# Sample queries in stretches of eight, three state slots, one masked copy a level

## The chip, the cores and the metric

The kernel runs on one core of one Trainium2 chip. The metric is the device time of one execution in microseconds (us), the median of the runs shown. The engines go by the names of the profile: PE (TensorE, the products), PEld (its weight loads), DVE (VectorE), ACT (ScalarE), POOL (GpSimd) and SP (SyncE, which issues most transfers).

## What is computed

One step of a decoder layer with two branches, for a prompt of 256 tokens and for 8 sequences with 4 new tokens each ("samples", 32 tokens), 288 tokens in all. Everything is float32.

```python
h = jnp.einsum('bld,de->ble', x, w_in)            # 2048 -> all projections
# gated linear attention (GLA): 4 heads, keys 256, values 512, a gate for each key
S_t = diag(a_t) S_{t-1} + k_t^T v_t ; o_t = q_t S_t
# retention: 8 heads, keys 128, values 256, one decay gamma a head
S_t = gamma S_{t-1} + k_t^T v_t ; o_t = q_t S_t
merged = sigmoid(ga) * rms(o_a) * silu(za) + sigmoid(gb) * groupnorm(o_b) * silu(zb)
y = jnp.einsum('ble,ed->bld', merged, w_out)
x_new = layer_norm(ALPHA * x + y)
```

The prompt starts from a zero state. The samples start from states that are inputs (16 GLA quads and 8 retention quads of 1 MB each in this kernel's layout), and the new states of both are outputs.

## The kernel before, in words

**The weight stream.** `w_in` is cut into 128 blocks of 128 columns, `w_out` into 16. A block is two halves of 512 KB. Each half is loaded by SyncE (line 228), split into a high and a low float32r part by ACT (line 244) and VectorE (line 245), and multiplied with the 288 tokens in three products for each 128 x 128 piece (lines 258 to 260), 48 products a block. Loads run six halves ahead, splits two halves ahead of the products.

**The order.** The program is written in the order in which every engine runs it; engines run in order. The main loop (line 1115) goes through the blocks a quarter (12 products) at a time. Before each quarter it calls `tick()`: every task (a Python generator) whose turn has come emits its next few instructions, and says with `yield n` in how many ticks it wants to go on. So attention work is laid between quarters of the weight stream, and a tick is one quarter. After the tick the next quarter is split, then multiplied. `Ring` hands out buffers in order: `get` waits tick by tick until the oldest buffer of a full ring is closed. The blocks come in four rounds j of 32; a round has the columns of one GLA head and two retention heads.

**GLA of the prompt.** `gla_main` (line 482) makes the 256 x 256 score matrix by levels: for m = 64, 32, ..., 2 the `producer` forms decayed queries `qs` and keys (lines 515 to 536), PE multiplies them (line 623), and `level_in` (line 596) puts the wanted entries into the scores `st` with two masked copies (`copy_predicated`, line 602), one for each of the two token blocks. The last level (m = 1), the diagonal, and the samples' own scores come out of `pairs` (line 542): POOL forms differences of decays and products of q and k, ACT the exponentials, VectorE multiplies them and adds the two key halves of 176 columns (lines 569, 570), POOL adds the two halves of the 288 diagonal columns (line 573) into `u`, and a product with ones sums over the partitions (line 578, 464 columns, f32). One tick later seven masked copies take the result out of PSUM (lines 581 to 592).

**GLA of the samples.** `gla_sample` (line 657) handles four state quads (j, kt, par). For each it forms a masked key tile `km` (VectorE, line 723), waits until the state's load was queued at least six ticks ago (`state_of`, line 287), lets two ticks go by, and multiplies the queries with the state: four products of 32 query columns with 512 state columns, each on its own 32 columns of the array and its own 32 partitions of `pos` (line 729, 128*32 in the profile). A tick later it begins the update: four times a product of `km` with v (line 734, float32r) into a buffer of the ring `po` (two buffers), and one tick later a VectorE operation (line 736) that decays the state and adds. Then `state_store` (line 292) stores the quad two ticks later and frees the slot; `state_loader` (line 277) queues the next load into the freed slot. `ret_sample` (line 873) does the same for retention quads, both halves par of a head in one quad (line 889, 256 columns; updates on lines 895 and 899). The ring `s8` has two slots, each of 8 KB a partition.

Of the kernel before, what the change touches and what calls it, by code (L numbers as in the profile page):

```python
# [14 lines left out]
ALU = mybir.AluOpType  # L15
# [84 lines left out]
def hybrid_step(ctx: ExitStack, tc: tile.TileContext, xT, xp, xs, w, wlra, wlr, cols, wo, lnwb, lnsb, sg, sr, cf, cu, dtab,  # L100
# [20 lines left out]
    S8 = Ring(spool, "s8", 2, [128, 2048])  # L121

    def R(tag, bufs, shape, dtype=F32, pool=None):
        return Ring(pool or apool, tag, bufs, shape, dtype)
# [8 lines left out]
    PU = R("pu", 1, [128, 2, 352])  # L133
    UU = R("uu", 1, [128, 464])
# [17 lines left out]
    SB = R("sb", 2, [128, NT])  # L152
# [329 lines left out]
    def gla_main(g):  # L482
# [31 lines left out]

        def produce(i):
# [4 lines left out]
            for t in range(2):  # L520
# [8 lines left out]
            dv, qv, kv = (x[:, :, 0:SEQ].rearrange("p k (i n h m) -> p k i n h m", i=2, h=2, m=m)  # L529
                          for x in (dd, q, k))  # L530
            for t in range(2):
                dve.tensor_tensor(qs[:, :, 64 * t:64 * t + 64].rearrange("p k (n m) -> p k n m", m=m),  # L532
                                  qv[:, :, t, :, 1 - t, :], dv[:, :, t, :, 1 - t, :], op=ALU.mult)
# [8 lines left out]
        def pairs():  # L542
# [3 lines left out]
            u = yield from UU.get()  # L546
            pf = p[:, :, 0:144]
            cv = c4.rearrange("p k i (n h) -> p k i n h", h=2)
            pool.tensor_tensor(p[:, :, 0:128].rearrange("p k (i n) -> p k i n", i=2), cv[:, :, :, :, 1],
                               cv[:, :, :, :, 0], op=ALU.subtract)  # L550
            cv = cs.rearrange("p k b (n h) -> p k (b n) h", h=2)
            pool.tensor_tensor(p[:, :, 128:144], cv[:, :, :, 1], cv[:, :, :, 0], op=ALU.subtract)
            for r in range(2):
                pool.tensor_tensor(p[:, :, 144 + 16 * r:160 + 16 * r].rearrange("p k (b t) -> p k b t", t=2),
                                   cs[:, :, :, 2:4], bc(cs[:, :, :, r:r + 1], [128, 2, DEC_BATCH, 2]),
                                   op=ALU.subtract)
            yield 1
            act.activation(p[:, :, 0:176], p[:, :, 0:176], AF.Abs)
            act.activation(p[:, :, 0:176], p[:, :, 0:176], AF.Exp, scale=-1.0 / TAU)
            kv = k.rearrange("p k (n h) -> p k n h", h=2)  # L560
            qv = q.rearrange("p k (n h) -> p k n h", h=2)
            for lo, hi, h in ((0, 64, 1), (64, 128, 0), (128, 144, 1)):
                pool.tensor_tensor(p[:, :, 176 + lo:176 + hi], qv[:, :, lo:hi, h], kv[:, :, lo:hi, 1 - h], op=ALU.mult)
            kv, qv = (x[:, :, SEQ:NT].rearrange("p k (b t) -> p k b t", t=DEC_SEQ) for x in (k, q))
            for r in range(2):
                pool.tensor_tensor(p[:, :, 320 + 16 * r:336 + 16 * r].rearrange("p k (b t) -> p k b t", t=2),
                                   qv[:, :, :, 2:4], bc(kv[:, :, :, r:r + 1], [128, 2, DEC_BATCH, 2]), op=ALU.mult)
# [10 lines left out]
            pe.matmul(pt[:, 0:464], lhsT=ones_t, rhs=u, start=True, stop=True)  # L578
            UU.close(u)
            yield 1  # L580
            dve.copy_predicated(st[:, 0:2, :], U("diag").rearrange("p (i t) -> p i t", i=2),
                                pt[:, 0:256].rearrange("p (i t) -> p i t", i=2))
            level_in(len(LEVELS) - 1, pt[:, 288:416])
            dve.copy_predicated(ss[:, 0, :, 0:8], U("sd").rearrange("p (g c) -> p g c", g=4),
# [3 lines left out]
                                pt[:, 416:432].rearrange("p (g n) -> p g n", g=4))  # L588
            sv = ss[:, 0, :, 0:8].rearrange("p g (n h m) -> p g n h m", h=2, m=2)
# [67 lines left out]
    def gla_sample(g):  # L657
# [61 lines left out]
        for kt in range(2):  # L719
            for par in range(2):  # L720
                qd = ("g", j, kt, par)
# [3 lines left out]
                s8 = yield from state_of(qd)  # L725
                s4 = s8.rearrange("p (g c) -> p g c", g=4)
                yield 2
                for gg in range(4):
                    pe.matmul(pos[32 * gg:32 * gg + 32, :], lhsT=qs[:, kt, 2 * gg + par, :], rhs=s4[:, gg, :],  # L729
                              start=kt + par == 0, stop=False)  # L730
                yield 1
                for gg in range(4):
# [3 lines left out]
                    dve.scalar_tensor_tensor(s4[:, gg, :], s4[:, gg, :], ecs[:, kt, gg, par, 3:4], po,  # L736
# [3 lines left out]
                spawn(state_store(s8, og_s[j, kt, par]))  # L740
# [132 lines left out]
    def ret_sample(r):  # L873
        j, kst, qs, vh = r.j, r.kst, r.qs, r.vh
        pos = yield from POS.get()
        for h in range(2):
# [5 lines left out]
            s4 = s8.rearrange("p (a g c) -> p a g c", a=2, g=4)  # L882
            for par in range(2):
# [694 lines left out]
```

## Time and profile before

| | us |
|---|---|
| median of 3 runs (1086.31 to 1088.1) | 1087.24 |
| profiled execution | 1086.71 |
| its span, first to last instruction | 1084.8 |
| PE busy | 1071.0 |
| DVE busy | 712.8 |
| ACT busy | 524.3 |
| POOL busy | 242.1 |

The profile is one execution. Times in its rows are counted from the first instruction. A PE row gives the start of a product and a modelled time until its end; products overlap, so the rows of PE add up to more than the span, and the distance between starts is what a product takes of the engine. A row with x8 is eight instructions without a gap between them; its time goes from the first start to the last end. An f32 product is two PE instructions, a float32r product one. The granted clock of PE is 0.998 of full over the span.

### The profile page before, as it was taken

The numbers are of one execution on the slowest core, as the hardware profiler recorded it, in microseconds if no ns is written. First come the engines' busy times: TensorE is split into PE (matmuls) and PEld (weight loads), VectorE is DVE, ScalarE is ACT, GpSimd is POOL, SyncE is SP. The second block draws the span as 40 slices with busy tenths as digits, with TensorE's granted clock in tenths as the row PEclk, the third lists the DMA queues.
The fourth block names the chain that finished last, engine by engine and source line by source line (L and its number), as shares of the span: only waits on it lengthen the run. The fifth ranks groups of instructions, "written<-read, shape, count | busy, mean of one in ns | idle before, by whom it ended". The sixth has DMA issues, their size and how long they took to land.

```text
span 1084.8 us, 20286 instructions
## 1 busy us (share of the span) xinstructions
PE 1071.0 (99%) x7987; PEld 1024.6 (94%) x7987; DVE 712.8 (66%) x1313; ACT 524.3 (48%) x1054; POOL 242.1 (22%) x345
## 2 busy tenths in 40 slices
PE   9999999999999999999999999999999999999996
PEld 7999999999999999999999999999989999999985
DVE  5758866655568767554578766554588667675557
ACT  6665344444565435344664444345564444453342
POOL 0223212121242213031260212040260221230003
PEclk9999999999999999999999999999999999999999
DMA  9744757575445776675436675664436774655853
GB/s 332 245 160 138 263 198 269 181 265 172 158 137 163 238 245 227 209 246 169 164 119 201 248 249 180 228 239 155 156 117 215 249 270 150 205 193 180 245 185 117
DMA packets 57807, 219.12 MB, mean 202 GB/s; under 512 B 6512, under 2 KB 8432, under 8 KB 51568
## 3 DMA queue, kind: packets, MB, share of 16 engines
q1 hardware_dynamic: 56288, 214.95, 58.4%
q10 hardware_dynamic: 1424, 2.88, 1.0%
q8 instruction: 63, 1.03, 0.4%
q14 instruction: 32, 0.26, 0.1%
HBM read 187.13 MB, written 30.67 MB: 201 GB/s over the span
## 4 chain that ended last, share of the span: by engine, by line
PE 96%; DVE 3%; DMA 0%; issue 0%; POOL 0%; ACT 0%; SPq 0%
PE acc L258 28%; PE acc L260 27%; PE acc L259 27%; PE pos L729 1%; PE po L734 1%; PE pt L309 1%; PE po L416 1%; PE po L414 1%; PE po L415 1%; PE pt L623 1%; PE pos L889 1%; PE po L895 1%; DVE wl L245 1%; DVE y L1348 1%; PE pt L352 0%; PE pt L383 0%
## 5 line engine op out<-in xcount | busy, mean ns | idle before, releaser
L258 PE MATMUL acc<-xh,wh 128*128 128x288 f32 x2240 | 673.9, 301 | 1.1 <-ACT wh L244 1.1
L259 PE MATMUL acc<-xl,wh 128*128 128x288 f32 x2240 | 660.6, 295 | 0.0
L260 PE MATMUL acc<-xh,wl 128*128 128x288 f32 x2240 | 659.5, 294 | 0.2 <-DVE wl L245 0.2
L245 DVE TENSOR_TENSOR wl<-raw,wh 128x512 fp32r<-128x512 f32 x572 | 408.4, 736 | 318.2 <-ACT wh L244 315.9
L244 ACT ACTIVATE wh<-raw 128x512 fp32r<-128x512 f32 x572 | 337.3, 625 | 435.2 <-PE acc L259 397.9
L258 PEld LDWEIGHTS acc<-xh,wh 128*128 128x128 f32 x2240 | 420.6, 188 | 22.4 <-issue 13.7
L259 PEld LDWEIGHTS acc<-xl,wh 128*128 128x128 f32 x2240 | 423.4, 189 | 3.5 <-issue 0.8
L260 PEld LDWEIGHTS acc<-xh,wl 128*128 128x128 f32 x2240 | 422.5, 189 | 0.5 <-DVE wl L245 0.4
L998 POOL TENSOR_TENSOR sg<-sg,sb 128x288 f32<-128x288 f32 x32 | 32.6, 1019 | 277.3 <-ACT sb L996 277.3
L736 DVE SCALAR_TENSOR_TENSOR s<-s,ec,po 128x512 f32<-128x512 f32 x64 | 47.4, 741 | 0.0
L761 POOL TENSOR_TENSOR kq<-t,t 64x288 f32<-64x288 f32 x16 | 15.9, 992 | 107.0 <-DVE t L755 106.4
L522 POOL TENSOR_TENSOR t<-cc 128x256 f32<-128x256 f32 x48 | 36.7, 794 | 0.0
L322 POOL TENSOR_SCALAR sm<-sm 128x1 f32<-128x1 f32 (+1 forms) x24 | 9.0, 376 | 105.7 <-ACT on L340 64.1
L734 PE MATMUL po<-vh,km 128*128 128x512 f32 x64 | 26.1, 408 | 1.8 <-DVE s L736 1.8
L899 DVE SCALAR_TENSOR_TENSOR s<-s,po 128x512 f32<-128x512 f32 x32 | 21.8, 680 | 3.1 <-PE po L895 3.1
L1331 POOL TENSOR_SCALAR mv<-mv 128x1 f32<-128x1 f32 x3 | 1.7, 559 | 96.3 <-DVE mv L1388 94.2
L532 DVE TENSOR_TENSOR qsc<-kq,t 128x128 f32<-128x128 f32 x48 | 22.4, 507 | 0.1
L665 POOL COPY qsp<-qe 128x32 f32<-128x32 f32 x8 | 4.6, 606 | 76.8 <-DVE qe L504 76.8
L470 POOL MEMSET t<- 128x4 f32 x4 | 0.4, 104 | 94.1 <-DVE t L464 77.8
L1206 ACT ACTIVATE y<-pt 128x256 f32<-128x256 f32 x12 | 4.6, 385 | 34.0 <-DVE stt L1203 24.6
L323 POOL TENSOR_TENSOR sm<-sm,cft 128x1 f32<-128x1 f32 (+1 forms) x24 | 19.2, 799 | 2.0
L919 POOL TENSOR_TENSOR merged<-merged,sg 128x288 f32<-128x288 f32 x16 | 15.5, 980 | 8.9 <-DVE merged L358 8.5
(257 smaller groups left out, 994.4 us busy)
## 6 DMA issues: line engine op xcount, KB each, us to landing
raw<-in_w SPq DMA_DIRECT2D x252, 512.0 KB, 4.3
s<-in_sg SPq DMA_DIRECT2D x16, 1024.0 KB, 4.9
out_og_s<-s SPq DMA_DIRECT2D x16, 1024.0 KB, 8.1
raw<-in_wo SPq DMA_DIRECT2D x32, 512.0 KB, 4.7
s<-in_sr SPq DMA_DIRECT2D x8, 1024.0 KB, 4.8
out_or_s<-s SPq DMA_DIRECT2D x8, 1024.0 KB, 6.6
raw<-in_w SPq DMA_DIRECT2D x8, 256.0 KB, 5.6
lnt<-in_lnwb ACTq DMA_DIRECT2D x4, 512.0 KB, 8.5
```

Source lines behind the costliest of these rows:

```text
L244: act.activation(a[:, s], t[:, s], AF.Copy)
L245: (pool if q in POOL_Q else dve).tensor_tensor(b[:, s], t[:, s], a[:, s].bitcast(F32), op=ALU.subtract)
L258: pe.matmul(acc, lhsT=a[:, k, :], rhs=xh, start=first and k == kk, stop=False)
L259: pe.matmul(acc, lhsT=a[:, k, :], rhs=xl, start=False, stop=False)
L260: pe.matmul(acc, lhsT=b[:, k, :], rhs=xh, start=False, stop=last and k == kk + 3)
L323: pool.tensor_tensor(r[:, 0:n], r[:, 0:n], bc(mhalf[:, 0:1], [128, n]), op=ALU.pow)
L522: pool.tensor_tensor(dd[:, :, t * 128:t * 128 + 128].rearrange("p k (n m) -> p k n m", m=2 * m), cv, bc(cv[:, :, :, m - 1 + t:m + t], [128 ...
L532: dve.tensor_tensor(qs[:, :, 64 * t:64 * t + 64].rearrange("p k (n m) -> p k n m", m=m), qv[:, :, t, :, 1 - t, :], dv[:, :, t, :, 1 - t, : ...
L734: pe.matmul(po, lhsT=km[:, gg, :], rhs=vh[:, 2, :], start=True, stop=True)
L736: dve.scalar_tensor_tensor(s4[:, gg, :], s4[:, gg, :], ecs[:, kt, gg, par, 3:4], po, op0=ALU.mult, op1=ALU.add)
L899: dve.scalar_tensor_tensor(sv, sv, g4, po, op0=ALU.mult, op1=ALU.add)
L998: pool.tensor_tensor(gt, gt, s, op=ALU.mult)
```

## The change

Sample queries: `gla_sample` takes the states of both par of one kt first and multiplies eight products in one stretch, before the first `km`; `ret_sample` does the same with the two halves of its quad. The waits of two ticks behind `km` stay, the tick behind the queries goes. The ring `s8` gets a third slot; for that `sb` gets one buffer in place of two, and `u` is dropped.

Levels: `level_in` makes one masked copy of 128 columns in place of two of 64, through a view (`half_view`) that reaches over both token blocks; the decayed queries are laid out for it, split by key half in place of token block.

The ones product: decays and products of `pairs` change places in `p`, which grows to 464 columns; VectorE's addition of 176 columns is dropped and POOL adds all 464; `p` itself is the operand of the ones product and is freed after it. The copies out of PSUM are spread over four ticks.

```diff
-    S8 = Ring(spool, "s8", 2, [128, 2048])
+    S8 = Ring(spool, "s8", 3, [128, 2048])
-    PU = R("pu", 1, [128, 2, 352])
-    UU = R("uu", 1, [128, 464])
+    PU = R("pu", 1, [128, 2, 464])
-    SB = R("sb", 2, [128, NT])
+    SB = R("sb", 1, [128, NT])
...
+        def half_view(ap, m):
+            return ap[:, m:m + 2 * (128 - m)].rearrange("p (i a m) -> p i a m", i=2, m=m)[:, :, ::2, :]
...
-            for t in range(2):
-                dve.tensor_tensor(qs[:, :, 64 * t:64 * t + 64].rearrange("p k (n m) -> p k n m", m=m),
-                                  qv[:, :, t, :, 1 - t, :], dv[:, :, t, :, 1 - t, :], op=ALU.mult)
+            for kt in range(2):
+                dve.tensor_tensor(qs[:, kt].rearrange("p (i n m) -> p i n m", i=2, m=m), half_view(q[:, kt], m),
+                                  half_view(dd[:, kt], m), op=ALU.mult)
...
-            dve.tensor_tensor(p[:, :, 0:176], p[:, :, 0:176], p[:, :, 176:352], op=ALU.mult)
-            dve.tensor_tensor(u[:, 288:464], p[:, 0, 0:176], p[:, 1, 0:176], op=ALU.add)
+            dve.tensor_tensor(dec, dec, qk, op=ALU.mult)
             pool.tensor_tensor(p[:, :, 0:NT], q, k, op=ALU.mult)
             yield 1
-            pool.tensor_tensor(u[:, 0:NT], p[:, 0, 0:NT], p[:, 1, 0:NT], op=ALU.add)
-            PU.close(p)
+            pool.tensor_tensor(p[:, 0], p[:, 0], p[:, 1], op=ALU.add)
             yield 2
             pt = yield from PT.get()
-            pe.matmul(pt[:, 0:464], lhsT=ones_t, rhs=u, start=True, stop=True)
-            UU.close(u)
+            pe.matmul(pt[:, 0:464], lhsT=ones_t, rhs=p[:, 0], start=True, stop=True)
+            PU.close(p)
             yield 1
             dve.copy_predicated(st[:, 0:2, :], U("diag")...
+            yield 1
             level_in(len(LEVELS) - 1, pt[:, 288:416])
+            yield 1
             dve.copy_predicated(ss[:, 0, :, 0:8], U("sd")...
             dve.copy_predicated(sv[:, :, :, 1], U("s1")...
+            yield 1
             for r in range(2):
                 dve.copy_predicated(sv[:, :, :, 1, :], U(f"s2{r}")...
...
         def level_in(i, src):
             m = LEVELS[i]
-            for t in range(2):
-                sv = st[:, t, :].rearrange("p (n h m) -> p n h m", h=2, m=m)
-                mk = U("lev")[:, i * 128 + 64 * t:i * 128 + 64 * t + 64].rearrange("p (n m) -> p n m", m=m)
-                dve.copy_predicated(sv[:, :, 1 - t, :], mk,
-                                    src[:, 64 * t:64 * t + 64].rearrange("p (n m) -> p n m", m=m))
+            sv = half_view(st.rearrange("p i t -> p (i t)"), m)
+            dve.copy_predicated(sv, U("lev")[:, i * 128:i * 128 + 128].rearrange("p (i n m) -> p i n m", i=2, m=m),
+                                src[:, 0:128].rearrange("p (i n m) -> p i n m", i=2, m=m))
...
         for kt in range(2):
+            s8 = []
             for par in range(2):
-                qd = ("g", j, kt, par)
+                t = yield from state_of(("g", j, kt, par))
+                s8.append(t)
+            s4 = [t.rearrange("p (g c) -> p g c", g=4) for t in s8]
+            for par in range(2):
+                for gg in range(4):
+                    pe.matmul(pos[32 * gg:32 * gg + 32, :], lhsT=qs[:, kt, 2 * gg + par, :], rhs=s4[par][:, gg, :],
+                              start=kt + par == 0, stop=False)
+            for par in range(2):
                 km = yield from KM.get()
                 E_KM.tensor_tensor(km, ...
-                s8 = yield from state_of(qd)
-                s4 = s8.rearrange("p (g c) -> p g c", g=4)
                 yield 2
-                for gg in range(4):
-                    pe.matmul(pos[32 * gg:32 * gg + 32, :], lhsT=qs[:, kt, 2 * gg + par, :], rhs=s4[:, gg, :],
-                              start=kt + par == 0, stop=False)
-                yield 1
                 for gg in range(4):
                     po = yield from PO.get()
                     pe.matmul(po, lhsT=km[:, gg, :], rhs=vh[:, 2, :], start=True, stop=True)
                     yield 1
...
             s8 = yield from state_of(qd)
+            for par in range(2):
+                for gg in range(4):
+                    pe.matmul(pos[32 * gg:32 * gg + 32, c], lhsT=qs[:, h, 2 * gg + par, :], rhs=s4[:, par, gg, :],
+                              start=h + par == 0, stop=False)
             for par in range(2):
                 km = yield from KM.get()
                 E_KM.tensor_tensor(km, ...
                 yield 2
-                for gg in range(4):
-                    pe.matmul(pos[32 * gg:32 * gg + 32, c], lhsT=qs[:, h, 2 * gg + par, :], rhs=s4[:, par, gg, :],
-                              start=h + par == 0, stop=False)
-                yield 1
                 for g2 in range(2):
```

## Rows read from the trace of the kernel before

**Rows 1.** The page, its first line and part 1 (busy us, share, instructions)

```profile
span 1084.8 us, 20286 instructions
...
PE 1071.0 (99%) x7987; PEld 1024.6 (94%) x7987; DVE 712.8 (66%) x1313; ACT 524.3 (48%) x1054; POOL 242.1 (22%) x345
```

**Rows 2.** Waits of PE: engine line waited for, us in total, times, longest

```profile
PE po L734 <- DVE s L736: 1.8, 1, 1.8
...
PE pt L578 <- POOL uu L573: 0.6, 1, 0.6
```

**Rows 3.** Timeline of PE around one GLA sample stretch: start us, us, engine line

```profile
135.31 0.29 PE L259 MATMUL acc<-xl,wh 128*128 128x288 f32 x1
135.44 0.29 PE L260 MATMUL acc<-xh,wl 128*128 128x288 f32 x1
135.67 1.07 PE L729 MATMUL pos<-s,qsp 128*32 128x512 f32 x8
136.66 0.40 PE L258 MATMUL acc<-xh,wh 128*128 128x288 f32 x1
136.90 0.29 PE L259 MATMUL acc<-xl,wh 128*128 128x288 f32 x1
```

**Rows 4.** The same stretch, window opened after its first four products ended

```profile
136.12 0.61 PE L729 MATMUL pos<-s,qsp 128*32 128x512 f32 x4
```

**Rows 5.** Timeline of PE around one retention sample stretch

```profile
201.77 0.29 PE L260 MATMUL acc<-xh,wl 128*128 128x288 f32 x1
201.99 0.64 PE L889 MATMUL pos<-s,qsp 128*32 128x256 f32 x8
202.56 0.40 PE L258 MATMUL acc<-xh,wh 128*128 128x288 f32 x1
202.80 0.29 PE L259 MATMUL acc<-xl,wh 128*128 128x288 f32 x1
```

**Rows 6.** The same retention stretch, window opened after its first four products

```profile
202.23 0.40 PE L889 MATMUL pos<-s,qsp 128*32 128x256 f32 x4
```

**Rows 7.** Groups by form on PE: busy us, mean ns of one, idle before

```profile
L729 PE MATMUL pos<-s,qsp 128*32 128x512 f32 x128 | 17.0, 605 | 0.0
...
L889 PE MATMUL pos<-s,qsp 128*32 128x256 f32 x128 | 10.2, 391 | 0.0
```

**Rows 8.** Timeline of VectorE in the fourth round

```profile
807.86 0.90 DVE L532 TENSOR_TENSOR qsc<-kq,t 128x128 f32<-128x128 f32 x2
...
809.20 0.44 DVE L581 COPY_PREDICATED st<-cut,pt 128x256 f32<-128x256 uint8 x1
809.67 0.45 DVE L602 COPY_PREDICATED st<-cut,pt 128x64 f32<-128x64 uint8 x2
...
810.76 0.69 DVE L245 TENSOR_TENSOR wl<-raw,wh 128x512 fp32r<-128x512 f32 x1
...
811.63 0.74 DVE L736 SCALAR_TENSOR_TENSOR s<-s,ec,po 128x512 f32<-128x512 f32 x1
```

**Rows 9.** Timeline of POOL ahead of the ones product, first round

```profile
83.56 1.75 POOL L571 TENSOR_TENSOR pu<-kq,kq 128x576 f32<-128x576 f32 x1 [3.90 <-DVE uu L570]
...
86.55 0.86 POOL L573 TENSOR_TENSOR uu<-pu 128x288 f32<-128x288 f32 x1
```

**Rows 10.** Timeline of VectorE in the same stretch

```profile
83.08 0.34 DVE L570 TENSOR_TENSOR uu<-pu 128x176 f32<-128x176 f32 x1
```

**Rows 11.** Timeline of PE at the ones product, first round

```profile
87.53 0.97 PE L578 MATMUL pt<-uu,ones_t 128*128 128x464 f32 x2
```

**Rows 12.** State loads (line 282): issue to landing, min/median/max

```profile
DMA to landing us min/median/max: 4.7/4.9/8.6
```

**Rows 13.** State stores (line 294): issue to landing, min/median/max

```profile
DMA to landing us min/median/max: 6.4/6.9/9.9
```

**Rows 14.** Timeline of SyncE, second round: the first state store

```profile
353.20 0.42 SPq L294 DMA_DIRECT2D out_og_s<-s  x1
```

**Rows 15.** Timeline of PE: the product that reads the load behind that store

```profile
374.25 0.64 PE L729 MATMUL pos<-s,qsp 128*32 128x512 f32 x4
```

More of the change, by code (lines that the diff above doesn't have):

```diff
@@ L528, in produce @@
             qs = yield from QSC.get()
-            dv, qv, kv = (x[:, :, 0:SEQ].rearrange("p k (i n h m) -> p k i n h m", i=2, h=2, m=m)
-                          for x in (dd, q, k))
-            for t in range(2):
-                dve.tensor_tensor(qs[:, :, 64 * t:64 * t + 64].rearrange("p k (n m) -> p k n m", m=m),
-                                  qv[:, :, t, :, 1 - t, :], dv[:, :, t, :, 1 - t, :], op=ALU.mult)
+            dv, kv = (x[:, :, 0:SEQ].rearrange("p k (i n h m) -> p k i n h m", i=2, h=2, m=m) for x in (dd, k))
+            for kt in range(2):
+                dve.tensor_tensor(qs[:, kt].rearrange("p (i n m) -> p i n m", i=2, m=m), half_view(q[:, kt], m),
+                                  half_view(dd[:, kt], m), op=ALU.mult)
             for t in range(2):
@@ L545, in pairs @@
             p = yield from PU.get()
-            u = yield from UU.get()
-            pf = p[:, :, 0:144]
+            dec, qk = p[:, :, 288:464], p[:, :, 0:176]
             cv = c4.rearrange("p k i (n h) -> p k i n h", h=2)
-            pool.tensor_tensor(p[:, :, 0:128].rearrange("p k (i n) -> p k i n", i=2), cv[:, :, :, :, 1],
+            pool.tensor_tensor(dec[:, :, 0:128].rearrange("p k (i n) -> p k i n", i=2), cv[:, :, :, :, 1],
                                cv[:, :, :, :, 0], op=ALU.subtract)
             cv = cs.rearrange("p k b (n h) -> p k (b n) h", h=2)
-            pool.tensor_tensor(p[:, :, 128:144], cv[:, :, :, 1], cv[:, :, :, 0], op=ALU.subtract)
+            pool.tensor_tensor(dec[:, :, 128:144], cv[:, :, :, 1], cv[:, :, :, 0], op=ALU.subtract)
             for r in range(2):
-                pool.tensor_tensor(p[:, :, 144 + 16 * r:160 + 16 * r].rearrange("p k (b t) -> p k b t", t=2),
+                pool.tensor_tensor(dec[:, :, 144 + 16 * r:160 + 16 * r].rearrange("p k (b t) -> p k b t", t=2),
                                    cs[:, :, :, 2:4], bc(cs[:, :, :, r:r + 1], [128, 2, DEC_BATCH, 2]),
@@ L557, in pairs @@
             yield 1
-            act.activation(p[:, :, 0:176], p[:, :, 0:176], AF.Abs)
-            act.activation(p[:, :, 0:176], p[:, :, 0:176], AF.Exp, scale=-1.0 / TAU)
+            act.activation(dec, dec, AF.Abs)
+            act.activation(dec, dec, AF.Exp, scale=-1.0 / TAU)
             kv = k.rearrange("p k (n h) -> p k n h", h=2)
@@ L562, in pairs @@
             for lo, hi, h in ((0, 64, 1), (64, 128, 0), (128, 144, 1)):
[L563 removed]
+                pool.tensor_tensor(qk[:, :, lo:hi], qv[:, :, lo:hi, h], kv[:, :, lo:hi, 1 - h], op=ALU.mult)
             kv, qv = (x[:, :, SEQ:NT].rearrange("p k (b t) -> p k b t", t=DEC_SEQ) for x in (k, q))
             for r in range(2):
[L566 removed]
+                pool.tensor_tensor(qk[:, :, 144 + 16 * r:160 + 16 * r].rearrange("p k (b t) -> p k b t", t=2),
                                    qv[:, :, :, 2:4], bc(kv[:, :, :, r:r + 1], [128, 2, DEC_BATCH, 2]), op=ALU.mult)
             yield 1
[L569 to L570 removed]
+            dve.tensor_tensor(dec, dec, qk, op=ALU.mult)
             pool.tensor_tensor(p[:, :, 0:NT], q, k, op=ALU.mult)
             yield 1
[L573 to L574 removed]
+            pool.tensor_tensor(p[:, 0], p[:, 0], p[:, 1], op=ALU.add)
             yield 2
             pt = yield from PT.get()
[L578 to L579 removed]
+            pe.matmul(pt[:, 0:464], lhsT=ones_t, rhs=p[:, 0], start=True, stop=True)
+            PU.close(p)
             yield 1
@@ L735, in gla_sample @@
                     yield 1
-                    dve.scalar_tensor_tensor(s4[:, gg, :], s4[:, gg, :], ecs[:, kt, gg, par, 3:4], po,
+                    dve.scalar_tensor_tensor(s4[par][:, gg, :], s4[par][:, gg, :], ecs[:, kt, gg, par, 3:4], po,
                                              op0=ALU.mult, op1=ALU.add)
@@ L739, in gla_sample @@
                 KM.close(km)
-                spawn(state_store(s8, og_s[j, kt, par]))
+                spawn(state_store(s8[par], og_s[j, kt, par]))
         EC.close(ec)
```

## The prediction

> **What bounds the kernel now.** I read the shares first: PE is busy 99% of the span and no other engine is near it [rows 1]. Then the waits of PE: two that the change can touch, 1.8 us on line 734 and 0.6 us on line 578, both in the fourth round [rows 2]. So the time is the sum of PE's own steps, plus about 2.4 us of waits here. A cheaper instruction on another engine gains nothing unless it ends one of these waits; a change pays if it takes steps off PE. What a step costs PE is the distance from one start to the next, since busy times of overlapping products hide it. Two weight products of 288 columns follow each other after 0.13 us, as the first two rows show [rows 3]. That is the yardstick.
>
> A sample stretch is read by the same distances. The last weight product before a GLA stretch starts at 135.44, the second one after it at 136.90: 1.46 us, where two plain steps would be 0.26. The stretch costs 1.20 us [rows 3]. Its eight PE instructions (each f32 product is run as two) come in two waves of four that run side by side, and the second wave starts at 136.12, 0.45 after the first [rows 3, 4]. Two waves are 0.90, so 0.30 us is the price of going from 128*128 products to 128*32 ones and back: 0.10 before the first, 0.09 behind the last wave, and 0.11 more before the second weight product. A retention stretch: 201.77 to 202.80 is 1.03, less 0.26 is 0.77; its waves are 0.24 apart (201.99, 202.23), so 0.48 is work and 0.29 is price [rows 5, 6].
>
> **The change, part by part.**
>
> *Stretches of eight.* Each f32 stretch now holds four products (eight instructions); 128 instructions on line 729 and 128 on line 889 make 16 + 16 stretches [rows 7]. They become 8 + 8, with the same products. What goes is 16 entries and exits: 8 x 0.30 + 8 x 0.29 = 4.7 us of PE, straight off the path. No row shows a third wave behind a second, the one thing that the saving hangs on. The nearest row is the second wave behind the first, 0.45 apart with nothing lost [rows 3, 4]; the far end is that the change of the product costs a whole exit and entry, and then the gain is 0. A gain beyond 4.7 is excluded, since the waves themselves stay. I take 4.7.
>
> *What moves with it.* In a GLA half (one kt) a stretch now comes before the first mask multiplication (line 723), and the tick behind each stretch goes: eight update products and eight updates (line 736) take about 12 ticks where they took 14. VectorE gets the same work more densely. In the fourth round VectorE is already late: the first update, 0.74 us at 811.63, ends at 812.4 and holds the third update product, which wanted to go 1.8 us earlier, at 810.6 (po has two buffers) [rows 2, 8]. In the new order the updates come one tick earlier, because the stretch no longer lies between mask and first update. Then the first update stands ahead of the level multiplications and copies that begin at 807.86 [rows 8]; it starts about 3.7 us sooner and the third product finds its buffer. The second update is the next late one: 807.9 + 0.65 for the first update, 1.3 for the multiplications (807.86 to 809.20), 0.47 for the diagonal copy (809.20 to 809.67), 0.6 for a split, 0.3 for a level copy and 0.65 for itself end at about 811.8 [rows 8]. PE wants it at about the place of the old third product, 810.6, pushed back by 0.3 (two more waves ahead of it, 0.9, less the 0.6 us wait that they swallow): 810.9. A wait of 0.9 us stays of 1.8. The 0.6 us before line 578 goes entirely, since PE arrives 0.9 us later there. Gain 0.9 + 0.6 = 1.5 us. Ends: 2.4 (both waits gone) and -1 (a wait as long as the old one, and another behind it).
>
> *One copy a level.* Two copies of 64 columns take 0.45 together where VectorE is crowded, one of 256 takes 0.44 [rows 8]; one of 128 lies between half of that and the whole, so it saves 0 to 0.2 us, 28 times, on an engine that is 66% busy [rows 1]. Its cover is VectorE's lead on PE; in the fourth round, where that is gone, three copies are 0.6 us at most. Taken as 0, it is inside the ends above.
>
> *The ones product.* VectorE loses the addition of 0.34 us (line 570) [rows 10]. POOL's addition (line 573) grows from 288 to 464 columns. From the two POOL rows, 1.75 us for 576 and 0.86 for 288, a column costs 3.1 ns, so 176 more are 0.54 us [rows 9]. POOL's multiplication waited for line 570 and starts 0.37 us earlier, so the addition ends 0.17 later. There is no cover: in the first round it ends at 87.41 and PE starts line 578 at 87.53 [rows 9, 11]. Allowing 0.05 us for the signal, PE waits about 0.1 us in each of three rounds: -0.3 us. Ends: 0 and -0.8 (0.27 each, if the 0.37 isn't regained because line 569 is late). The Trainium skill (GPSIMD Engine Reference, Elementwise, side-by-side cycle accounting) gives about 2.6 cycles an element for a two-input operation; at the 1.2 GHz it names, 176 would cost an estimated 0.38 us, the addition would end at its old time, and this term would be 0. The rows of this case say 3.1 ns, and they decide.
>
> *Copies over four ticks.* They come three ticks later in part. Behind them wait the levels' use of pt (three buffers, taken in order): a level may be read one tick later. No PE product waits for the masks until the scores are split many ticks on. 0, with the third free pt buffer as the cover; if that fails, levels shift by a tick (1.59 us = 12 x 0.13 of PE work that goes on meanwhile), and PE loses nothing.
>
> *Third state slot, one sb buffer.* The slot is what lets two states be held while a third loads. The single sb buffer is rewritten two blocks (8 ticks) after its last reader: 0. The number of state loads and stores is the same, and each load still waits on SyncE for the store of its slot, with weight loads queued behind it, as now. What is new is how soon a load is used. Now the product of the third quad comes 8 ticks after its load is queued (6 in state_of, 2 behind the mask). In the new order the stretch of the second kt goes 6 ticks after the load of its second state. In the second round the first store issues at 353.20 and the product starts at 374.25: 21.1 us [rows 14, 15]. Take off two ticks (3.2) and the stretch that no longer lies between (1.2): 16.7 us are left for a store and a load, which need 6.9 + 4.9 = 11.8 by the medians and 9.9 + 8.6 = 18.5 if both are the slowest of the run [rows 12, 13]. I take 0; the ends are 0 and -1.8 a round.
>
> **Sum.** -4.7 - 1.5 + 0.3 = -5.9 us. The profiled execution took 1086.7 us (span 1084.8 [rows 1] and 1.9 around it), so 1080.8; the median of the runs shown is 1087.24, 0.5 above it, so I forecast 1081.3 us.
>
> **Rivals.**
>
> *The third wave pays.* If the change from one state's products to the next costs PE what an exit and an entry cost, the 4.7 goes and 1.5 - 0.3 = 1.2 us is left: 1086.0. For it: no row has such a change. Against it: the two waves that are shown already change weights without loss [rows 3, 4]. Chance 0.10.
>
> *VectorE falls behind in every round.* The denser updates meet the level multiplications in rounds one to three too, and each round gets a wait like the one of the fourth, 1.8 us: three of these less the gain of 5.9 is -0.5, so 1086.7. For it: the two-buffer chain of update product and update is the same in each round, and one such wait exists [rows 2]. Against it: VectorE's wait shows in one round of four, and the scattered copies take a burst off the place. Chance 0.12, a third of it with waits small enough to stay faster.
>
> *The state comes too late: slower.* At the stretch of each second kt PE stands with its whole queue behind it until the second state has landed. Each us beyond 16.7 costs one us, four times. It decides from 16.7 + 5.9/4 = 18.2 us between store and landing; at 19.5 in every round the time is 1087.24 + 4 x 1.3 = 1092.4, 1.3 being the part past 18.2. For it: stores and loads now lie closer, and the slowest of each would make 18.5 [rows 12, 13]. Against it: by the medians 5 us are spare. Chance 0.08, of which 0.05 slower.
>
> **How the numbers follow.** Forecast 0.70 (waits in the fourth round that go or stay included), rivals 0.10, 0.12 and 0.08. A measurement of this kernel can tell about 0.2%, 2.2 us, from no change: faster is below 1085.1, slower above 1089.4. The forecast's own range (1079.8 with all waits gone, 1084 with half of the wave saving) is all faster; with a third of the second rival and a little of the others: faster 0.80. Same: most of the first two, 0.15. Slower 0.05. The range runs from 1079.5 to 1086.0, which reaches into the first rival and leaves the slower cases out.
>
> **What would show it.** Right: PE's timeline has 16 stretches of sixteen f32 instructions in four waves 0.45 (GLA) and 0.24 (retention) apart, and each costs 2.1 and 1.25 us between weight products instead of twice 1.20 and 0.77; the wait on line 736 shrinks to about 1 us and the one on line 573 in the fourth round is gone; starts of line 578 lag the 12th weight product by 0.1. Wrong: a gap inside the stretches ahead of the third wave; waits of the update products in rounds one to three; a wait of the fifth product of a stretch for a state load.

## The result and the profile after

| | before | after |
|---|---|---|
| median, us | 1087.12 | 1079.80 |
| lowest to highest, 4 runs each | 1086.31 to 1088.1 | 1079.67 to 1081.15 |
| span of the profiled execution, us | 1084.8 | 1077.9 |

The ratio is 0.9932, with an interval of 0.9920 to 0.9944: 7.3 us faster, where the forecast was 5.9 (from 1087.24, the median of three runs, to 1081.3). 1079.80 lies in the stated range of 1079.5 to 1086.0, close to its fast end. The page of the changed kernel, its first line and part 1, answers to [rows 1]:

```profile
span 1077.9 us, 20256 instructions
...
PE 1067.2 (99%) x7987; PEld 1026.9 (95%) x7987; DVE 707.5 (66%) x1281; ACT 524.4 (49%) x1054; POOL 240.8 (22%) x345
```

PE does the same 7987 instructions and is still busy 99% of the span. The waits of PE, in us in total, times and longest, answer to [rows 2]:

```profile
PE pt L1016 <- POOL qe L1013: 1.1, 1, 1.1
PE acc L257 <- ACT wh L243: 0.2, 1, 0.2
PE po L737 <- DVE s L739: 0.2, 1, 0.2
```

Of the 1.8 us on the update product (now line 737) 0.2 is left, and the wait before the ones product is gone; the wait of 1.1 us lies ahead of the first round in every kernel here.

The timeline of PE around a GLA stretch (start us, us, then engine, line and tile), to be held against [rows 3]:

```profile
130.52 0.29 PE L259 MATMUL acc<-xh,wl 128*128 128x288 f32 x1
130.74 1.92 PE L728 MATMUL pos<-s,qsp 128*32 128x512 f32 x16
132.60 0.40 PE L257 MATMUL acc<-xh,wh 128*128 128x288 f32 x1
132.84 0.30 PE L258 MATMUL acc<-xl,wh 128*128 128x288 f32 x1
```

The same stretch, window opened after its first eight instructions ended:

```profile
131.63 1.04 PE L728 MATMUL pos<-s,qsp 128*32 128x512 f32 x8
```

From 130.52 to 132.84 are 2.32 us; less two plain steps, 0.26, the stretch costs 2.06. The third wave, the first with the other state, starts at 131.63: 0.89 after the first, no more than twice the 0.45 between a first and a second wave [rows 3, 4]. It costs no more than a second wave. A retention stretch, against [rows 5]:

```profile
180.42 0.29 PE L259 MATMUL acc<-xh,wl 128*128 128x288 f32 x1
180.64 1.07 PE L889 MATMUL pos<-s,qsp 128*32 128x256 f32 x16
181.65 0.40 PE L257 MATMUL acc<-xh,wh 128*128 128x288 f32 x1
181.88 0.29 PE L258 MATMUL acc<-xl,wh 128*128 128x288 f32 x1
```

1.46 less 0.26 is 1.20 us.

**Where the time came from.** The weight products are the same 6720 in the same order in every kernel here, so the starts of the nth one in two traces tell how far one is behind the other at that place. Taken at the ends of the first three rounds and, for the fourth, at the last weight product, this is what each kernel loses (+) or gains (-) against the changed kernel in each round, in us; "start" is what had come about by 37 us (the fourth block), which stays the same until 86 us, before the first sample stretch (97 us):

| kernel | start | round 1 | round 2 | round 3 | round 4 | median |
|---|---|---|---|---|---|---|
| before | -0.03 | 1.12 | 1.14 | 1.07 | 3.62 | 1087.1 |
| the changed kernel again (after_pair) | 0.90 | 0.00 | 0.00 | 0.00 | 0.25 | 1080.51 |
| only_stretch | -0.10 | 0.95 | 0.96 | 0.98 | 1.45 | 1083.8 |
| no_stretch | -0.02 | 1.26 | 1.34 | 1.26 | 2.33 | 1085.95 |
| cut_stretch | 0.58 | 1.90 | 1.90 | 1.91 | 1.09 | 1086.69 |
| burst | -0.24 | 0.94 | 0.91 | 0.94 | 1.28 | 1083.7 |
| late_burst | -0.21 | 0.00 | 0.00 | 0.00 | -0.31 | 1080.08 |
| two_copies | 0.61 | 0.00 | 0.00 | 0.00 | 0.18 | 1080.6 |
| add_back | 0.26 | 0.00 | 0.00 | 0.00 | 0.19 | 1079.86 |
| two_slots | -0.18 | -0.05 | -0.05 | -0.05 | 1.98 | 1082.71 |
| ret16 | -0.22 | -0.29 | -0.29 | -0.29 | -0.29 | 1079.16 |
| ret16_pair | -0.18 | -0.29 | -0.29 | -0.29 | 0.21 | 1078.58 |

Two executions of the changed kernel differ by 0.9 us before the first round and by 0.25 in the last, and by 0.00 in the three between: rounds one to three can be read to hundredths, the start not at all, and the fourth round to about 0.25.

### The profile page after: what moved, and what is told of

It is laid out like the page before. It is cut to its first block, busy times and chain, and to the rows that moved or that the text cites. A ratio compares the mean times of both kernels' runs of the same rounds, so it can differ in the third digit from the quotient of the medians.

```text
span 1077.9 us, 20256 instructions
## 1 busy us (share of the span) xinstructions
PE 1067.2 (99%) x7987; PEld 1026.9 (95%) x7987; DVE 707.5 (66%) x1281; ACT 524.4 (49%) x1054; POOL 240.8 (22%) x345
## 4 chain that ended last, share of the span: by engine, by line
PE 95%; DVE 3%; DMA 0%; POOL 0%; issue 0%; ACT 0%; SPq 0%; POOLq 0%
PE acc L257 27%; PE acc L259 27%; PE acc L258 27%; PE po L737 1%; PE pos L728 1%; PE po L413 1%; PE po L415 1%; PE po L414 1%; PE pt L623 1%; PE pt L308 1%; PE pos L889 1%; PE po L899 1%; DVE wl L244 1%; DVE y L1352 1%; DMA raw<-in_w 0%; PE pt L351 0%
## 5 line engine op out<-in xcount | busy, mean ns | idle before, releaser
L244 DVE TENSOR_TENSOR wl<-raw,wh 128x512 fp32r<-128x512 f32 x572 | 404.3, 730 | 318.3 <-ACT wh L243 316.0
L764 POOL TENSOR_TENSOR kq<-t,t 64x288 f32<-64x288 f32 x16 | 15.8, 989 | 105.3 <-DVE t L758 104.7
```

The lines of the kernel that those rows point to most:

```text
L244: (pool if q in POOL_Q else dve).tensor_tensor(b[:, s], t[:, s], a[:, s].bitcast(F32), op=ALU.subtract)
```

## The experiments

**1. The stretches alone, all but the stretches, and a cut between the fours.** How does the gain divide between the stretches and the other edits? By the prediction the merges are 4.7 us whatever else is done, and the copies are worth nothing; by its rivals a third wave, or updates that VectorE can't follow, take the 4.7 back.

only_stretch is the kernel before with nothing but the new stretches, the third slot and the single sb buffer (`u` is laid into `p`, which is freed after the ones product; the additions are those of before):

```diff
-    S8 = Ring(spool, "s8", 2, [128, 2048])
+    S8 = Ring(spool, "s8", 3, [128, 2048])
+            for par in range(2):
+                s8.append((yield from state_of(("g", j, kt, par))))
...
             for par in range(2):
                 km = yield from KM.get()
```

> The kernel before with the stretches of eight, the third state slot and the single sb buffer alone; masked copies, levels and the ones product are as before. Theory A (the gain is 16 saved changes between 128*128 and 128*32 products, 0.29 us each, and in the fourth round the updates that come ahead of the copies): rounds one to three gain 1.1 to 1.2 us each, as in the changed kernel, the fourth at least 3: about 1080.5 us. Theory B (the fourth round's part comes from the cheaper and scattered copies): rounds one to three the same, the fourth 1.2 to 1.8: about 1082.2 us.

no_stretch is the changed kernel with stretches of four, as before:

```diff
+                s8 = yield from state_of(qd)
                 yield 2
+                for gg in range(4):
+                    pe.matmul(pos[32 * gg:32 * gg + 32, :], ...)
+                yield 1
                 for gg in range(4):
```

> The changed kernel with the sample products put back into stretches of four behind each mask; copies, levels, ones product and slots are as changed. Theory A: rounds one to three as before the change (0 +- 0.1 us), the fourth gains at most 1 us: 1086 to 1087. Theory B: the fourth round gains 2 to 2.5 us by itself: about 1084.7.

cut_stretch is the changed kernel with a tick between the two fours:

```diff
             for par in range(2):
+                if par:
+                    yield 1
                 for gg in range(4):
                     pe.matmul(pos[32 * gg:32 * gg + 32, ...
```

> The changed kernel with one tick (a quarter of the weight stream) between the first and the second four products of every stretch, nothing else. Theory A: each of the 16 cuts brings back one exit and one entry, 0.29 us: 16 x 0.29 = 4.6 us longer, about 1084.4, and PE's timeline shows 32 stretches that cost 1.20 and 0.77 us again. Rival (the gain of rounds one to three is the new order, not the changes of the product's shape): 1079.8 +- 0.5.

Measured: only_stretch 1083.8 us (ratio to before 0.997, 0.996 to 0.9981), no_stretch 1085.95 (0.9991, 0.9981 to 1.0), cut_stretch 1086.69 (0.9997, 0.9988 to 1.0007). The span of only_stretch is 2.7 us below that of before, that of no_stretch 0.7; together 3.4, of the 6.9 that the whole change took. So the parts need each other. The waits of PE in only_stretch say why:

```profile
PE po L735 <- DVE s L737: 3.8, 4, 1.5
```

Four waits of the update products for VectorE, one a round, where before had one. The merges are there (where no other product lies beside them its stretches cost 2.05 and 1.19 us, as in the changed kernel), and the waits take them back: rounds one to three gain 0.10 to 0.18 us each where the changed kernel gains 1.07 to 1.14. cut_stretch goes on at the other end. A tick between the fours puts back the four entries and exits of a round, 4 x 0.29 = 1.16 us (its stretches cost about 1.20 and 0.77 again), and delays the updates, so that waits come back here too (0.5 each at 123.41, 362.77 and 602.10):

```profile
PE po L739 <- DVE s L741: 1.5, 3, 0.5
```

1.16 and 0.5 are 1.66 of the 1.90 that it loses in each of these rounds; of the other 0.24, 0.1 to 0.2 is what a wait costs beyond its row (experiment 2). Neither number expected of only_stretch came, and cut_stretch lost more than its expectation had, both for the same reason: the updates' waits in rounds one to three. no_stretch missed its expectations as well: rounds one to three are 0.14 to 0.20 us longer than in the kernel before, with no wait of PE, and the fourth gains 1.29 where at most 1, or 2 to 2.5, was expected. What costs it the 0.14 to 0.20 isn't shown.

**2. Which part keeps VectorE ahead.** Three candidates: the copies over four ticks, the one copy a level, the addition taken off VectorE. Each was undone alone in the changed kernel.

burst, the seven copies in one tick:

```diff
             yield 1
             dve.copy_predicated(st[:, 0:2, :], U("diag")...
-            yield 1
             level_in(len(LEVELS) - 1, pt[:, 288:416])
-            yield 1
             dve.copy_predicated(ss[:, 0, :, 0:8], U("sd")...
...
-            yield 1
             for r in range(2):
```

> The changed kernel with one edit: the seven masked copies behind the ones product are issued in one tick again, as in the kernel before; stretches of eight, three slots, one copy a level and the longer POOL addition stay. Theory A (the spreading is what keeps the updates from waiting): with the stretches alone the fourth update product of each round waits 0.74 to 1.49 us (121.16, 359.56, 598.00, 812.13), because the last level copy (118.14) and the split behind it (119.17) stand ahead of the second update on VectorE; in the changed kernel the last level copy comes a tick later (119.26), behind the second update (118.01). Then the burst brings the waits back: rounds one to three lose 0.7 to 1.0 us each, the fourth 1.0 to 1.5, and the median is 1083.0 to 1084.2. Theory B (the shorter copies and the dropped addition do it): no wait over 0.3 us comes back and the median stays at 1079.8 within 0.5. Theory C (it is for the fourth round alone, as the prediction's rivals had it): only the wait of the fourth round comes back, 1081 to 1081.5.

two_copies, with level_in as it was before:

```diff
-            sv = half_view(st.rearrange("p i t -> p (i t)"), m)
-            dve.copy_predicated(sv, ...)
+            for t in range(2):
+                sv = st[:, t, :].rearrange("p (n h m) -> p n h m", h=2, m=m)
+                dve.copy_predicated(sv[:, :, 1 - t, :], ...)
```

> The changed kernel with one edit: each level goes into the scores with two masked copies of 64 columns in place of one of 128 (0.35 to 0.45 us for the two against 0.30 for the one); all else stays, the spreading too. Theory A (the order of the copies matters, not their length): the median stays at 1079.8 within 0.5, and no update product waits over 0.4 us; in the fourth round the 0.16 us gap at 807.97 may grow by 0.1 to 0.2. Theory B (the length matters): the update products of rounds one to three wait 0.7 to 0.8 us again, and the median is 1082 or more.

add_back, with VectorE's addition of 176 columns and POOL's of 288 (`u` is here the first half of `p`):

```diff
+            dve.tensor_tensor(u[:, 288:464], p[:, 0, 0:176], p[:, 1, 0:176], op=ALU.add)
-            pool.tensor_tensor(p[:, 0], p[:, 0], p[:, 1], op=ALU.add)
+            pool.tensor_tensor(u[:, 0:NT], p[:, 0, 0:NT], p[:, 1, 0:NT], op=ALU.add)
```

> The changed kernel with one edit: VectorE adds the 176 columns of the two key halves again and POOL only the 288 of the diagonal, as before. My prediction put a price of 0.3 us on the moved addition (POOL at 3.1 ns a column, so PE late at the ones product by 0.1 us in three rounds); the trace of the changed kernel shows 0.40 us more on POOL, begun 0.43 to 0.49 earlier, and no wait. Theory A (the move costs and gains nothing): 1079.8 within 0.5. Theory B (the addition of 0.34 us on VectorE is part of what made the updates late): waits of 0.2 to 0.4 us come back, in the fourth round above all, 1080.2 to 1081.5. Theory C (the prediction's term was right): 0.3 us faster than the changed kernel.

Measured: burst 1083.7 us (0.9969, 0.9957 to 0.9981), two_copies 1080.6 (0.9940, 0.9925 to 0.9955), add_back 1079.86 (0.9933, 0.9917 to 0.9950). Only the burst brings the waits back, all four of them; this is the line of its waits of PE:

```profile
PE po L734 <- DVE s L736: 3.7, 4, 1.4
```

What changed is seen on VectorE, in the timeline of burst at the first of these waits:

```profile
116.73 0.75 DVE L736 SCALAR_TENSOR_TENSOR s<-s,ec,po 128x512 f32<-128x512 f32 x1
...
117.99 0.44 DVE L599 COPY_PREDICATED st<-cut,pt 128x128 f32<-128x128 uint8 x1
119.02 0.56 DVE L397 TENSOR_TENSOR stl<-st,sth 128x384 fp32r<-128x384 f32 x1 [0.59 <-ACT sth L396]
119.59 0.58 DVE L300 TENSOR_TENSOR ssh<-ss,ssh 32x128 fp32r<-32x128 f32 x2
120.21 0.75 DVE L736 SCALAR_TENSOR_TENSOR s<-s,ec,po 128x512 f32<-128x512 f32 x1
```

and on PE in the same stretch:

```profile
119.98 0.29 PE L259 MATMUL acc<-xh,wl 128*128 128x288 f32 x1
121.01 0.50 PE L734 MATMUL po<-vh,km 128*128 128x512 f32 x1 [0.74 <-DVE s L736]
121.35 0.29 PE L257 MATMUL acc<-xh,wh 128*128 128x288 f32 x1
```

Between the first and the second update stand the last level copy (117.99) and the split of the scores behind it, which itself waits 0.59 us for ACT. The second update ends at 120.96, and the product that needs its po buffer starts at 121.01. The same stretch of VectorE in the changed kernel:

```profile
116.74 0.75 DVE L739 SCALAR_TENSOR_TENSOR s<-s,ec,po 128x512 f32<-128x512 f32 x1
...
118.01 0.74 DVE L739 SCALAR_TENSOR_TENSOR s<-s,ec,po 128x512 f32<-128x512 f32 x1
...
119.26 0.45 DVE L602 COPY_PREDICATED st<-cut,pt 128x128 f32<-128x128 uint8 x1
120.30 0.56 DVE L397 TENSOR_TENSOR stl<-st,sth 128x384 fp32r<-128x384 f32 x1 [0.59 <-ACT sth L396]
...
121.49 0.75 DVE L739 SCALAR_TENSOR_TENSOR s<-s,ec,po 128x512 f32<-128x512 f32 x1
```

The last level copy comes a tick later, behind the second update, which ends 2.2 us sooner. The copy, the split and its wait for ACT are the same work; they stand at another place in the queue. This is PE in the changed kernel at the place of the wait:

```profile
120.25 0.30 PE L259 MATMUL acc<-xh,wl 128*128 128x288 f32 x1
120.39 0.39 PE L737 MATMUL po<-vh,km 128*128 128x512 f32 x1
120.61 0.30 PE L257 MATMUL acc<-xh,wh 128*128 128x288 f32 x1
```

From the start of the weight product ahead to the start of the one behind are 1.37 us in burst and 0.36 here: 1.01 for a wait whose row says 0.74. The row counts from the modelled end of the product ahead, and without a wait that end overlaps the next product. The rounds agree: burst loses 0.94, 0.91 and 0.94 in the first three, for rows of 0.74, 0.83 and 0.74. So here a wait costs 0.1 to 0.2 us more than its row.

two_copies and add_back lose 0.18 and 0.19 us, in the fourth round alone, less than the 0.25 between two executions of one kernel. 0.15 and 0.13 of it lie in the stretch near 829, which took 2.07 and 2.05 us where the changed kernel's took 1.92; its state landed at 830.63 and 830.29, after the third wave's due place (0.89 behind 829.67 and 829.35), as in the second execution of the changed kernel (see the third slot below). What is left for the two parts themselves is under 0.1 us.

**3. Later, or broken up?** The spread copies do two things: no burst, and the PSUM buffer is held three ticks longer, so that the levels behind it come later. late_burst keeps the second without the first: all seven copies in the last of the four ticks.

```diff
             pe.matmul(pt[:, 0:464], lhsT=ones_t, rhs=p[:, 0], start=True, stop=True)
-            yield 1
+            yield 4
             dve.copy_predicated(st[:, 0:2, :], U("diag")...
...
```

> The changed kernel with its copies behind the ones product in one tick again, but in the last of the four ticks: the PSUM buffer is held as long as in the changed kernel, and the burst is as dense as in the kernel before. With the burst in the first tick (1083.7 us) the fourth update product of each round waits 0.74 to 1.40 us. Theory A (what counts is that the levels behind it come a tick later, through the PSUM buffer, so that the last level copy and the split stand behind the second update): the last level copy of the first round stands behind the second update (near 118.0) again, no wait over 0.3 us in rounds one to three, and 1079.8 to 1081; the burst may cost up to 1 us in the fourth round, where it meets the updates. Theory B (what counts is that the burst is broken up): the waits of rounds one to three stay at 0.7 to 0.8 us, 1083 to 1084.

Measured: 1080.08 us (0.9938, 0.9921 to 0.9954), with no wait of an update product in any round. On its VectorE the order is that of the changed kernel:

```profile
117.80 0.74 DVE L736 SCALAR_TENSOR_TENSOR s<-s,ec,po 128x512 f32<-128x512 f32 x1
...
119.06 0.44 DVE L599 COPY_PREDICATED st<-cut,pt 128x128 f32<-128x128 uint8 x1
```

So a burst as dense as the old one does no harm in a later tick. What pays is that the levels come later. In the fourth round, too, the burst at its late place costs nothing: it stands behind the first four updates there, and the round is 0.31 us shorter than in the changed kernel, 0.16 of it the wait that the changed kernel has left.

**4. What the third slot pays for.** two_slots is the changed kernel with two state slots.

```diff
-    S8 = Ring(spool, "s8", 3, [128, 2048])
+    S8 = Ring(spool, "s8", 2, [128, 2048])
```

> The changed kernel with a ring of two state slots in place of three. It measures what the third slot pays for. The first state of a kt leaves its slot at the store of 114.98 and a load lands in it at 127.26, before the stretch of the second kt (130.74); the second state is stored at 126.37, and the load behind it lands at 139.77. With two slots the stretch needs both loads. Theory A (PE stands until the second load has landed): about 9 us more in each round at this place, and as much again where the next head's states are wanted soon, so 36 us or more in all: 1116 to 1150. Theory B (the six ticks of the loader and the order of the tasks move the stretch later together with its state, and weight products go on meanwhile): the median rises by less than 3 us.

Measured: 1082.71 us (1081.37 to 1084.18; 0.9960, 0.9945 to 0.9975). The stretch of the second kt moves behind its loads (from 130.74 to 140.52 in the first round) and weight products go on meanwhile: rounds one to three lose nothing. The fourth does, as its timeline of PE shows:

```profile
840.24 1.06 PE L728 MATMUL pos<-s,qsp 128*32 128x512 f32 x8
843.00 1.06 PE L728 MATMUL pos<-s,qsp 128*32 128x512 f32 x8 [1.69 <-DMA s<-in_sg]
```

and the timeline of SyncE's queue ahead of it:

```profile
828.06 0.51 SPq L293 DMA_DIRECT2D out_og_s<-s  x1
838.00 0.33 SPq L281 DMA_DIRECT2D s<-in_sg  x1
```

From the issue of the store to the products are 14.9 us, and PE stands 1.7 us for the load behind it. In this execution (1081.41 us) the third slot buys about 2 us, all in the fourth round. Two of the four runs took 1084.0 and 1084.2 us, and no trace shows what they waited for; by the medians the slot buys 2.9 us, so Theory B (less than 3) holds, but barely.

**5. One stretch more.** If an entry and an exit have a price of their own, both retention heads in one stretch of sixteen take four more away. ret16 was run twice, the second time beside the changed kernel on the same chip.

```diff
+        for h in range(2):
+            held.append((yield from state_of(("r", 2 * j + h))))
...
         for h in range(2):
-            s8 = yield from state_of(qd)
```

> The changed kernel with the two retention heads of a round taken together: both states are waited for, then sixteen products (32 instructions, eight waves) in one stretch. Theory A: four more changes saved, 4 x 0.29 = 1.2 us: 1078.6. Rival: the second state of the pair comes so late that the round's sample work moves, with waits of PE for the load: 1079.8 or more.

> The changed kernel itself, as a base on the same chip for the two runs beside it: 1079.8 us within 0.5.

> The changed kernel with both retention heads of a round in one stretch of sixteen, beside the changed kernel on the same chip: four entries and exits less, at 0.29 us each, are 1.15 us; the first look had 1.37 us less in the span, 0.22 of it at the start. If the price is one of the entry and exit alone, 1.0 to 1.4 us faster than the changed kernel; if the first look was the start's chance, within 0.3.

Measured: 1079.16 us the first time (0.9926, 0.9911 to 0.9941), then 1078.58 (0.9922, 0.9907 to 0.9937) beside 1080.51 of the changed kernel (0.9939, 0.9924 to 0.9953). The timeline of PE around one of its stretches:

```profile
180.24 0.29 PE L259 MATMUL acc<-xh,wl 128*128 128x288 f32 x1
180.46 1.93 PE L888 MATMUL pos<-s,qsp 128*32 128x256 f32 x32
182.33 0.40 PE L257 MATMUL acc<-xh,wh 128*128 128x288 f32 x1
182.56 0.29 PE L258 MATMUL acc<-xl,wh 128*128 128x288 f32 x1
```

Eight waves in 2.32 - 0.26 = 2.06 us. By the table each merge is 0.29 us, in all four rounds of the first run. (The stretches' own rows would make it 0.34, twice 1.20 less 2.06; where the other 0.05 goes isn't shown.) This version is below both kernels in both runs, by its medians 0.6 and 1.9 us below the changed kernel. The start blurs the second number: of the 1.98 us between the two profiled executions 1.08 lie ahead of the first round and aren't its doing. In its second run the fourth round gave 0.5 us back against the first run. 0.3 of it is this wait of PE, for a state that landed 14.3 us after its slot's store was issued (815.00 to 829.27):

```profile
PE pos L728 <- DMA s<-in_sg: 0.3, 1, 0.3
```

## Why the prediction held, point by point

**Stretches of eight, -4.7 us: right.** Sixteen merges at 0.29 are 4.6. The unknown on which it hung, the third wave, costs nothing: it comes 0.89 after the first, though the state changes there. The stretches cost 2.06 and 1.20 us where 2.1 and 1.25 were forecast. The first rival (the third wave pays) is out.

**Round 4, -1.5 us: right in kind, too small.** The fourth round gained 3.62 us; less four merges 2.5, of which 2.2 are waits that went (2.4 [rows 2], 0.16 left). The other 0.3 is about what two waits cost beyond their rows, at 0.1 to 0.2 each (experiment 2). I had 0.9 us of the wait stay. This trace runs 3.3 us ahead of the old one there, so the first update, forecast at 807.9, should start at 804.6, and the second should end at 808.5. VectorE in the fourth round of the changed kernel:

```profile
804.57 0.75 DVE L739 SCALAR_TENSOR_TENSOR s<-s,ec,po 128x512 f32<-128x512 f32 x1
805.24 0.49 DVE L534 TENSOR_TENSOR qsc<-kq,t 128x128 f32<-128x128 f32 x2
805.64 0.49 DVE L537 TENSOR_TENSOR t<-kq,t 128x128 f32<-128x128 f32 x2
806.04 0.45 DVE L580 COPY_PREDICATED st<-cut,pt 128x256 f32<-128x256 uint8 x1
...
807.17 0.75 DVE L739 SCALAR_TENSOR_TENSOR s<-s,ec,po 128x512 f32<-128x512 f32 x1
```

The product that waited for the second update, on PE:

```profile
807.97 0.50 PE L737 MATMUL po<-vh,km 128*128 128x512 f32 x1 [0.16 <-DVE s L739]
```

The first update is where it was put, to 0.03 us, and the queue behind it is the one I wrote down. The term that was mis-sized is the level multiplications: 0.80 us from 805.24 to 806.04, where I took 1.3 from [rows 8]; the copies behind them make the other 0.1. With that the second update ends at 807.92 and not 808.5, PE comes for it at 807.8 and not 807.6, and 0.16 us are left of 0.9.

**Copies over four ticks, "0, PE loses nothing": wrong, and the largest error of the text.** I did see that levels may shift by a tick, but asked only what PE loses by it. I should have asked what stands ahead of the updates without the shift. Put back, the burst costs 0.94, 0.91, 0.94 and 1.28 us, 4.1 in all. The second rival (VectorE falls behind in every round) was thus a true mechanism, at 0.74 to 0.83 us of wait in rounds one to three and not 1.8: the denser stretches do bring it on, and this part of the same change takes it away. My ground against that rival, that the scattered copies "take a burst off the place", named the right edit and the wrong reason, since late_burst shows that the burst may stay. The sum came out by luck, because I left out the wait and its cure together.

**One copy a level, 0: it stands**, within the 0.25 us of the fourth round. The copy of 128 columns takes 0.29 to 0.45 us.

**The ones product, +0.3 us: wrong in size, 0.** POOL in the first round, where [rows 9] had 86.55 and 0.86 for the addition:

```profile
83.07 1.81 POOL L571 TENSOR_TENSOR pu<-kq,kq 128x576 f32<-128x576 f32 x1 [3.26 <-DVE pu L570]
...
86.12 1.26 POOL L573 TENSOR_TENSOR pu<-pu 128x464 f32<-128x464 f32 x1
```

and PE at the ones product, against [rows 11]:

```profile
87.56 0.94 PE L577 MATMUL pt<-pu,ones_t 128*128 128x464 f32 x2
```

The 176 further columns took 0.40 us, not 0.54. My 3.1 ns a column is the difference between two kinds of instruction, a multiplication over two halves of 288 columns (1.75 us) and an addition of 288 (0.86) [rows 9]; the same addition at 288 and at 464 columns gives 2.3 ns. Why the multiplication takes more isn't shown. The multiplication starts 0.49 us earlier, and the addition ends at 87.38 where it ended at 87.41. The Trainium skill's price (GPSIMD Engine Reference, Elementwise, side-by-side cycle accounting: about 2.6 cycles an element) gave an estimated 0.38 and a term of 0; the trace agrees with both.

**Third slot, 0, and the third rival (the state comes too late): it did not decide, but the cushion was thinner than I said.** I had 16.7 us from a store to the stretch, worked out in the second round and taken for all four. In the second round of the changed kernel it is 15.7 (352.45 to 368.18), in the first 114.98 to 130.74, 15.8 us; this is SyncE there:

```profile
114.98 0.42 SPq L293 DMA_DIRECT2D out_og_s<-s  x1
122.37 0.33 SPq L281 DMA_DIRECT2D s<-in_sg  x1
```

In the fourth round it is 13.0 (store 816.06, stretch 829.02), or 13.9 to the third wave of the stretch, which is the first to read this state. Loads and stores took, issue to landing (min, median, max), against [rows 12, 13]:

```profile
DMA to landing us min/median/max: 4.7/4.9/9.0
...
DMA to landing us min/median/max: 6.5/7.4/10.7
```

Store and load together took 11.7 to 12.8 us at the four places. The wait needs no worst case, though: in the second execution of the changed kernel this state landed 14.0 us after the store's issue (816.95 to 830.97), and the stretch in the fourth round took 2.15 us in place of 1.92. These are its rows in the first and the second execution:

```profile
829.02 1.92 PE L728 MATMUL pos<-s,qsp 128*32 128x512 f32 x16
...
829.92 2.15 PE L728 MATMUL pos<-s,qsp 128*32 128x512 f32 x16
```

That is the 0.25 of its row in the table.

**The sum.** -4.6 for the merges, -2.2 for the waits by their rows and -0.3 beyond them, 0 for the ones product: 7.1, of which rounds one to three fall 0.15 short (3.33 gained for twelve merges, 3.48). That makes the 6.9 us between the spans.

## What to carry to other kernels

Where an edit packs the work of an in-order engine more densely, write down what stands in its queue between two steps of the dependent chain, in every round; an edit that only moves such work by a tick can be worth as much as the one that the change is named for. Take the price of more columns from two lengths of the same instruction, not from two instructions of different kinds. A cushion that was measured in one round holds for that round: look for the place where it is smallest, here the fourth round, with 13.0 us against 15.8.

## What the runs showed of the hardware

Joining two stretches of 128*32 products into one saved 0.27 to 0.29 us each time, from two waves to four and from four to eight. So going from 128*128 products to 128*32 products and back costs about that, however many waves lie between, and the rows show no cost of a change of the operand or the state between waves. A 1 MB state that is stored and replaced by another through the same slot took between 11.7 and 14.9 us at the places read, 11.7 and 14.0 at the same place in two executions of one kernel. So the stretch of the fourth round, whose third wave had 2.1 us to spare in one execution (landed 827.80, wave at 829.91), waits in some executions and not in others. A wait of PE cost 0.1 to 0.2 us more than its row says (0.91 to 0.94 for rows of 0.74 to 0.83). And with the same instructions two executions differ by up to 0.9 us before the first round and then by 0.00 over three rounds, which is why comparisons here were read round by round.
